# A decoder step on one core: last output in two token halves, dt copied as its output ends, C projected from token 12

## The chip, the cores and the metric

One Trainium2 chip, one of its cores. The metric is the device time of one execution in microseconds; the kernel before has a median of 880.47 over 3 runs (879.78 to 883.48).

## The reference, cut to what matters

One layer of a hybrid decoder for 304 tokens: 16 learned meta tokens, 256 prompt tokens and 8 sample sequences of 4 tokens. `mix` stands for the short gated convolution (branch A) and the state-space scan (branch B), both fed by one input projection.

```
h = x + 0.5 * swiglu(rmsnorm(h0), w_gu1) @ w_down1
u = rmsnorm(h) @ w_in        # A_b | A_c | A_h | z | xBC | dt | gate_A | gate_B
xbc = silu(causal_dwconv4(xBC) + bias)     # x: 16 tiles of channels, B: 4, C: 4
h = h + mix(u) @ w_o
h = h + 0.5 * swiglu(rmsnorm(h), w_gu2) @ w_down2
y = rmsnorm(h)               # without the meta tokens
```

D is 1024 (8 tiles of 128 channels), the hidden width 2816 (22 tiles). The rows of C for the 16 meta tokens are read only by the convolution (width 4) of the tokens behind them: no output for a meta token is wanted, and the scan reads C from token 16.

## The kernel before, in words

Channels lie on partitions and tokens along the free axis. Every weight tile of 128x128 is used once, in the order of a written list (`program`, line 68): an entry names a phase (`g1`, `dt`, `x`, `d2`, ...), an output tile m and a step k. `drive` (line 232) walks through it. Eight weight tiles make a unit that comes with one load on SP (`w_dma`, four units ahead) and is cast in two parts (`split_piece`, line 178, three units ahead): ScalarE writes `whi`, VectorE the rest `wlo`. Both are of a rounded fp32 type (fp32r), as the two parts of the activations are. Each entry is three matmuls (lines 255 to 257): high by high, high by low, low by high. They accumulate in one PSUM tile per output; the pool for these has four buffers (`psm`), another of four serves the scan and the norms (`pss`). When an output ends, its handler is called (`ev_x`, `ev_d`, ...). The order on each engine is set by a scheduler of the framework, which starts from the order of the program but may move instructions.

Beside the list runs `side`, a queue of generators that `drive` steps through at a rate per entry (`RATE1` 0.15 in the `x` phase). The dt output is handled there: its handler (line 593) only appends the generator `setup` (line 726), whose first step copies the PSUM tile to `dtraw` (line 735).

In the `x` phase outputs come in pairs, first B with C of a group, and `ev_x` (line 484) copies them to `cb`, convolves them (lines 495 to 499) and writes `xs`. Each matmul covers the columns in `spans`: 304 for `x`, 288 for phases that need no meta tokens.

The end: `d2` has 8 outputs of 22 steps each. `ev_d` (line 386) adds each to the residual stream `h` and calls `last_chunk` (line 684): a square and a running sum for the final norm (`square_chunk`), and `hn`, which is `h` times the norm's weight. For m=7 evict and square are done in two halves of 144 tokens. Behind the last matmul come two calls of `finish` (line 695; the sums over channels as plain fp32 matmuls, the root, two VectorE steps, in `rms`), five multiplications of `hn` by the norm (line 699) and five stores (line 700).

Of the kernel before, what the change touches and what calls it, by code (L numbers as in the profile page):

```python
# [34 lines left out]
XC = 16  # L35
XBC = XC + 2 * G
EPS = 1e-6
UT = 8
NWARM = 8
AHEAD = {"1": 2, "2": 1}  # L40
# [81 lines left out]
def tile_step(ctx: ExitStack, tc: tile.TileContext, wst: bass.AP, xT: bass.AP, vec: bass.AP,  # L122
# [102 lines left out]

    operands = {}
    spans = {}
    handlers = {}
    ps_t = {}
    wanted = {"rate": 0.0, "due": 0.0}  # L230

    def drive(ph_stop=None, m_stop=None):

        i = clock["i"]
        while i < len(PROGRAM):
            e = PROGRAM[i]
            if e[1] == ph_stop and (m_stop is None or e[2] == m_stop):
                break
            if e[0] == "mm":
                _, ph, m, k, first, last = e  # L240
                t = clock["t"]
                u, s = divmod(t, UT)
                if s == 0:
                    w_dma(u + LD)
                    w_split(u + LS)
                c0, c1 = spans[ph]
                if first:

                    pl, tag = (pss, "s") if ph in ("g1", "u1") and m == AHEAD["1"] else (psm, "m")
                    ps_t[ph, m] = pl.tile([P, 512], F32, name=f"ps_{ph}{m}", tag=tag)  # L250
                o = ps_t[ph, m][:, :c1 - c0]
                wh = hi_t[u][:, s * P:(s + 1) * P]
                wl = lo_t[u][:, s * P:(s + 1) * P]
                xh, xl = operands[ph](m, k)
                te.matmul(o, lhsT=wh, rhs=xh, start=first, stop=False)  # L255
                te.matmul(o, lhsT=wh, rhs=xl, start=False, stop=False)  # L256
                te.matmul(o, lhsT=wl, rhs=xh, start=False, stop=last)  # L257
                clock["t"] = t + 1
                run_due()
                wanted["due"] = min(wanted["due"] + wanted["rate"], 1.0 * len(side))  # L260
                while wanted["due"] >= 1.0:
                    wanted["due"] -= 1.0
                    side_step()
            else:
                _, ph, m = e
                c0, c1 = spans[ph]
                handlers[ph](m, ps_t.pop((ph, m))[:, :c1 - c0])
            i += 1
        clock["i"] = i
# [89 lines left out]
            return [q[:, k, c0:] for q in un]  # L359


    def ffn(i, norm, fp, hook, parts=None):

        c0, n = norm.c0, norm.n
        parts = parts or ((0, n),)
        spans.update({"g" + i: (c0, T), "u" + i: (c0, T), "d" + i: (c0, T)})
        hh = fp.tile([P, FC, n], F32R, name="hh" + i)
        hl = fp.tile([P, FC, n], F32R, name="hl" + i)
        sg = {}

        def ev_g(j, ps):
            s = fp.tile([P, n], F32, name=f"sg{i}_{j}", tag="sg", bufs=2)
            q = fp.tile([P, n], F32, name=f"sgr{i}_{j}", tag="hid", bufs=2)
            dve.tensor_tensor(out=q, in0=ps, in1=norm.r, op=ALU.mult)
            act.activation(s, q, AF.Silu)
            dve.tensor_tensor(out=s, in0=s, in1=norm.r, op=ALU.mult)
            sg[j] = s

        def ev_u(j, ps):
            s = sg.pop(j)  # L380
            q = fp.tile([P, n], F32, name=f"hid{i}_{j}", tag="hid", bufs=2)
            dve.tensor_tensor(out=q, in0=ps, in1=s, op=ALU.mult)
            act.activation(hh[:, j, :], q, AF.Copy)
            dve.tensor_tensor(out=hl[:, j, :], in0=q, in1=hh[:, j, :].bitcast(F32), op=ALU.subtract)

        def ev_d(m, ps):
            for a, b in parts if m == DC - 1 else ((0, n),):
                o = h[:, m, c0 + a:c0 + b]
                dve.scalar_tensor_tensor(out=o, in0=ps[:, a:b], scalar=0.5, in1=o, op0=ALU.mult, op1=ALU.add)
                hook(m, a, b)  # L390

        operands["g" + i] = operands["u" + i] = lambda m, k: norm.get(True, k, c0)
        operands["d" + i] = lambda m, k: (hh[:, k, :], hl[:, k, :])
        handlers["g" + i], handlers["u" + i], handlers["d" + i] = ev_g, ev_u, ev_d
# [89 lines left out]
    def ev_x(m, ps):  # L484
        b = cb[len(pair)]
        sb = blocks(b, 3 + S0, 7)
        act.activation(b[:, 3:3 + S0], ps[:, 0:S0], AF.Copy)
        act.activation(sb[:, :, 3:7], blocks(ps, S0, NT), AF.Copy)
        pool.tensor_copy(sb[:, :, 0:3], hs_t[:, m])
        c = xp.tile([P, CW], F32, name=f"cv{m}", tag="cv", bufs=4)  # L490
        pair.append((m, b, c))
        if len(pair) < 2:
            return
        for m, b, c in pair:
            act.activation(c[:, :CN], b[:, 0:CN], AF.Copy, scale=vcol(V_CW + 4 * m))
        for q in range(1, 4):
            for m, b, c in pair:
                dve.scalar_tensor_tensor(out=c[:, :CN], in0=b[:, q:q + CN], scalar=vcol(V_CW + 4 * m + q),
                                         in1=c[:, :CN], op0=ALU.mult, op1=ALU.add)
        for m, b, c in pair:  # L500
            pool.tensor_copy(ocs[:, m], tails(b, S0, 7, 3))
        both = list(pair)
        pair.clear()
# [1 line left out]
        cb.append(cb.pop(0))  # L505

        def last():
            for m, b, c in both:
                bias = vcol(V_CB + m)
                act.activation(xs[:, m, 0:S0], c[:, 0:S0], AF.Silu, bias=bias)  # L510
                act.activation(blocks(xs[:, m, :], S0, NT), blocks(c, 3 + S0, 7)[:, :, 0:NT], AF.Silu, bias=bias)
            ssd.bc = ssd.bc or both[1][0] == 1
        after(1, last)
# [56 lines left out]
                  "ga": (NM, T), "ya": (NM, T), "z": (NM, T), "gb": (NM, T), "yb": (NM, T), "wo": (NM, T)})  # L570
    for ph in ("x", "dt", "ac", "ah", "ab", "ga", "z", "gb"):
        def op(m, k, ph=ph):
            return nmx.get(ph == "ga" and m < nraw, k, spans[ph][0])
        operands[ph] = op
    operands["ya"] = lambda m, k: (ya[0][:, k, :], ya[1][:, k, :])
    drive("dt")
# [13 lines left out]


    ssd = Scan(tc, mp, pss, dram, xs, V, K, h0, o_hp, o_hs)
    dt_box["fn"] = lambda ps: side.append(ssd.setup(ps, xp))
    wanted["rate"] = RATE1
    drive("ac")
    run_due(True)
# [86 lines left out]

    def last_chunk(m, a, b):
        nf.chunk(m, a, b)
        if b == TM:
            act.activation(hn[:, m, :], h[:, m, NM:], AF.Copy, scale=vcol(V_NF + m))

    halves = ((0, TM // 2), (TM // 2, TM))
    ffn("2", n2, fp, last_chunk, halves)  # L690
    drive()
    run_due(True)

    for a, b in halves:
        nf.finish(a, b)

    for i, (m0, m1) in enumerate(((0, 1), (1, 2), (2, 4), (4, 6), (6, DC))):
        o = hn[:, m0:m1, :]
        dve.tensor_tensor(out=o, in0=o, in1=nf.r.unsqueeze(1).to_broadcast([P, m1 - m0, TM]), op=ALU.mult)
        (nc.scalar if i % 2 else nc.sync).dma_start(o_y[:, m0:m1], o)  # L700
    f_st.close()
    raw_st.close()
    h_st.close()
# [2 lines left out]
class Scan:  # L706
# [16 lines left out]
        self.n += 1  # L723
        return self.sp.tile(shape, dt, name=f"{name}_{self.n}", tag=tag or name, bufs=bufs)

    def setup(self, psd, xp):

        nc, K, V = self.nc, self.K, self.V  # L730
        te, act, dve, pool = nc.tensor, nc.scalar, nc.vector, nc.gpsimd
        ident = K[:, C_ID:C_ID + P]
        raw = xp.tile([P, T], F32, name="dtraw")
        reps = xp.tile([P, 2, P], F32, name="dtrep")
        act.activation(raw, psd, AF.Copy)  # L735
        act.activation(reps[:, 0].rearrange("p (k t) -> p k t", t=NL),
                       raw[:, TL:S0].unsqueeze(1).to_broadcast([P, P // NL, NL]), AF.Copy)
        act.activation(reps[:, 1].rearrange("p (k t) -> p k t", t=NB * NT),
# [502 lines left out]
```

## Time and profile before

| | |
|---|---|
| median of 3 runs | 880.47 us |
| profiled execution, its own time | 881.86 us |
| span of the profiled execution | 880.0 us |
| TensorE matmuls busy | 868.8 us (99%) |
| VectorE busy | 621.3 us (71%) |
| ScalarE busy | 496.2 us (56%) |
| mean granted clock of TensorE | 0.996 |

The span runs from the first to the last instruction of the profiled execution. In rows, PE is a matmul on TensorE, PEld its weight load, DVE is VectorE, ACT ScalarE, SPq and ACTq the issue of DMAs. L257 is line 257 of the kernel. Matmuls overlap, so a row shows one longer than the distance to the next.

### The profile page before, as it was taken

What the parts mean: (1) busy time and instruction counts of PE and PEld (TensorE: products, weight loads), DVE (VectorE), ACT (ScalarE), POOL (GpSimd) and SP (SyncE); (2) the same over time, 40 slices, a digit from 0 to 9 for tenths busy, and PEclk for the clock granted to TensorE, in tenths of its full rate; (3) what the DMA queues carried; (4) which work ended last, traced back from release to release, by engine and by line L of the source; (5) the groups of instructions that cost most, each with busy time, mean ns of one, the idle gap of its engine ahead of it and who ended that gap; (6) DMA issues with size and microseconds to landing.
All of it is one profiled execution on the core that took longest, in us unless ns stands there. A gap on an engine that the chain in (4) does not pass through costs nothing.

```text
span 880.0 us, 16239 instructions
## 1 busy us (share of the span) xinstructions
PE 868.8 (99%) x6448; PEld 849.8 (97%) x6448; DVE 621.3 (71%) x996; ACT 496.2 (56%) x899; POOL 53.4 (6%) x86
## 2 busy tenths in 40 slices
PE   9999999999999999999999999999999999999996
PEld 7999999999999999999999899999999999999996
DVE  6756666554677798799988999886676666665443
ACT  8543434343667787966655687774465444444442
POOL 0000000000012233001000211100000000000000
PEclk9999999999999999999999999999999999999999
DMA  8554545454644545865666655755555555555541
GB/s 299 190 155 157 165 147 167 146 166 150 201 166 146 153 153 171 314 211 202 231 223 225 242 198 174 257 183 169 167 168 166 164 165 166 163 164 168 169 139 54
DMA packets 45851, 158.69 MB, mean 180 GB/s; under 512 B 7168, under 2 KB 9504, under 8 KB 43472
## 3 DMA queue, kind: packets, MB, share of 16 engines
q1 hardware_dynamic: 45344, 157.21, 54.6%
q8 instruction: 50, 0.82, 0.4%
q10 hardware_dynamic: 432, 0.46, 0.2%
q14 instruction: 25, 0.20, 0.1%
HBM read 145.34 MB, written 12.31 MB: 179 GB/s over the span
## 4 chain that ended last, share of the span: by engine, by line
PE 97%; DVE 1%; ACT 1%; DMA 1%; SPq 0%; issue 0%; DVEq 0%
PE ps_d L257 6%; PE ps_d L256 5%; PE ps_d L255 5%; PE ps_u L257 5%; PE ps_g L255 5%; PE ps_u L256 5%; PE ps_u L255 5%; PE ps_g L257 5%; PE ps_g L256 5%; PE ps_x L255 3%; PE ps_x L256 3%; PE ps_x L257 3%; PE ps_z L255 2%; PE ps_z L257 2%; PE ps_yb L257 2%; PE ps_yb L255 2%
## 5 line engine op out<-in xcount | busy, mean ns | idle before, releaser
L184 DVE TENSOR_TENSOR wlo<-wraw,whi 128x1024 fp32r<-128x1024 f32 (+2 forms) x250 | 300.6, 1204 | 188.8 <-ACT whi L183 188.1
L183 ACT ACTIVATE whi<-wraw 128x1024 fp32r<-128x1024 f32 (+2 forms) x250 | 259.6, 1041 | 296.8 <-issue 182.8
L257 PE MATMUL ps_d<-hh,wlo 128*128 128x304 f32 (+1 forms) x352 | 105.6, 300 | 0.0
L255 PE MATMUL ps_d<-hh,whi 128*128 128x304 f32 (+1 forms) x352 | 105.0, 299 | 0.0
L256 PE MATMUL ps_d<-hl,whi 128*128 128x304 f32 (+1 forms) x352 | 104.7, 298 | 0.0
L256 PEld LDWEIGHTS ps_d<-hl,whi 128*128 128x128 f32 x352 | 66.7, 189 | 0.0
L257 PEld LDWEIGHTS ps_d<-hh,wlo 128*128 128x128 f32 x352 | 66.2, 188 | 0.0
L255 PEld LDWEIGHTS ps_d<-hh,whi 128*128 128x128 f32 x352 | 66.1, 188 | 0.0
L255 PE MATMUL ps_x<-unh,whi 128*128 128x304 f32 x192 | 58.8, 309 | 0.7 <-ACT dtraw L735 0.7
L256 PE MATMUL ps_x<-unl,whi 128*128 128x304 f32 x192 | 58.8, 307 | 0.0
L257 PE MATMUL ps_x<-unh,wlo 128*128 128x304 f32 x192 | 58.6, 306 | 0.0
L255 PE MATMUL ps_g<-n1h,whi 128*128 128x304 f32 x176 | 54.1, 308 | 0.7 <-ACT whi L183 0.7
L256 PE MATMUL ps_u<-n1l,whi 128*128 128x304 f32 x176 | 53.6, 304 | 0.0
L255 PE MATMUL ps_u<-n1h,whi 128*128 128x304 f32 x176 | 53.5, 304 | 0.0
L256 PE MATMUL ps_g<-n1l,whi 128*128 128x304 f32 x176 | 53.4, 304 | 0.0
L257 PE MATMUL ps_g<-n1h,wlo 128*128 128x304 f32 x176 | 53.1, 303 | 0.0
L257 PE MATMUL ps_u<-n1h,wlo 128*128 128x304 f32 x176 | 52.9, 302 | 0.0
L257 PE MATMUL ps_g<-n2h,wlo 128*128 128x288 f32 x176 | 52.3, 297 | 0.0
L255 PE MATMUL ps_u<-n2h,whi 128*128 128x288 f32 x176 | 52.2, 297 | 0.0
L257 PE MATMUL ps_u<-n2h,wlo 128*128 128x288 f32 x176 | 52.1, 296 | 0.0
L255 PE MATMUL ps_g<-n2h,whi 128*128 128x288 f32 x176 | 51.9, 295 | 0.0
L256 PE MATMUL ps_u<-n2l,whi 128*128 128x288 f32 x176 | 51.4, 292 | 0.0
(342 smaller groups left out, 2435.6 us busy)
## 6 DMA issues: line engine op xcount, KB each, us to landing
wraw<-wst SPq DMA_DIRECT2D x241, 512.0 KB, 3.5
h<-h SPq DMA_DIRECT2D x8, 1024.0 KB, 5.0
o_hs<-h SPq DMA_DIRECT2D x8, 1024.0 KB, 4.3
acb<-cumd SPq DMA_DIRECT2D x8, 512.0 KB, 4.3
wraw<-wst SPq DMA_DIRECT2D x7, 256.0 KB, 6.4
hd<-h SPq DMA_DIRECT2D x1, 1216.0 KB, 6.6
h<-hd SPq DMA_DIRECT2D x1, 1216.0 KB, 8.3
o_hp<-hf SPq DMA_DIRECT2D x8, 128.0 KB, 2.8
```

The source lines that it names most:

```text
L183: act.activation(hi[:, a:b], r[:, a:b], AF.Copy)
L184: dve.tensor_tensor(out=lo[:, a:b], in0=r[:, a:b], in1=hi[:, a:b].bitcast(F32), op=ALU.subtract)
L255: te.matmul(o, lhsT=wh, rhs=xh, start=first, stop=False)
L256: te.matmul(o, lhsT=wh, rhs=xl, start=False, stop=False)
L257: te.matmul(o, lhsT=wl, rhs=xh, start=False, stop=last)
```

## The change

- The last output (`d2`, m=7) is made in two halves of the tokens: 66 matmuls of 144 columns for the first, then 66 for the second, from the same weight tiles, which are kept, into a PSUM tile of its own. After six of the 22 steps of the second half `out(0, TH)` is called: norm, two multiplications and two stores (both on SP) for the first half. Behind the last matmul come the norm, four multiplications and four stores for the second half.
- The handler of dt copies the PSUM tile to `dtraw` itself; the generator starts with the copy.
- The four outputs for C cover the columns from token 12 (292 instead of 304); copies, convolution and activation of these are cut to match.

```diff
--- before.py
+++ after.py
@@ -35,6 +35,7 @@
 XC = 16
 XBC = XC + 2 * G
 EPS = 1e-6
+C0 = NM - 4
 UT = 8
 NWARM = 8
 AHEAD = {"1": 2, "2": 1}
@@ -225,9 +226,20 @@
 
     operands = {}
     spans = {}
+
+    def span(ph, m):
+        return (C0, T) if ph == "x" and m >= XC + G else spans[ph]
+
     handlers = {}
     ps_t = {}
+    byhalf = {}
     wanted = {"rate": 0.0, "due": 0.0}
+
+    def three(o, ws, xs, cols, first, last):
+        (wh, wl), (xh, xl) = ws, [x[:, cols] for x in xs]
+        te.matmul(o, lhsT=wh, rhs=xh, start=first, stop=False)
+        te.matmul(o, lhsT=wh, rhs=xl, start=False, stop=False)
+        te.matmul(o, lhsT=wl, rhs=xh, start=False, stop=last)
 
     def drive(ph_stop=None, m_stop=None):
 
@@ -243,7 +255,19 @@
                 if s == 0:
                     w_dma(u + LD)
                     w_split(u + LS)
-                c0, c1 = spans[ph]
+                c0, c1 = span(ph, m)
+                if (ph, m) in byhalf:
+
+                    (a, b), kept = byhalf[ph, m]
+                    if first:
+                        ps_t[ph, m] = psm.tile([P, 512], F32, name=f"ps_{ph}{m}a", tag="m")
+                    ws = [t[u][:, s * P:(s + 1) * P] for t in (hi_t, lo_t)]
+                    kept.append((ws, operands[ph](m, k)))
+                    three(ps_t[ph, m][:, a:b], *kept[-1], slice(a, b), first, last)
+                    clock["t"] = t + 1
+                    run_due()
+                    i += 1
+                    continue
                 if first:
 
                     pl, tag = (pss, "s") if ph in ("g1", "u1") and m == AHEAD["1"] else (psm, "m")
@@ -263,7 +287,7 @@
                     side_step()
             else:
                 _, ph, m = e
-                c0, c1 = spans[ph]
+                c0, c1 = span(ph, m)
                 handlers[ph](m, ps_t.pop((ph, m))[:, :c1 - c0])
             i += 1
         clock["i"] = i
@@ -359,10 +383,8 @@
             return [q[:, k, c0:] for q in un]
 
 
-    def ffn(i, norm, fp, hook, parts=None):
-
+    def ffn(i, norm, fp, hook):
         c0, n = norm.c0, norm.n
-        parts = parts or ((0, n),)
         spans.update({"g" + i: (c0, T), "u" + i: (c0, T), "d" + i: (c0, T)})
         hh = fp.tile([P, FC, n], F32R, name="hh" + i)
         hl = fp.tile([P, FC, n], F32R, name="hl" + i)
@@ -383,11 +405,10 @@
             act.activation(hh[:, j, :], q, AF.Copy)
             dve.tensor_tensor(out=hl[:, j, :], in0=q, in1=hh[:, j, :].bitcast(F32), op=ALU.subtract)
 
-        def ev_d(m, ps):
-            for a, b in parts if m == DC - 1 else ((0, n),):
-                o = h[:, m, c0 + a:c0 + b]
-                dve.scalar_tensor_tensor(out=o, in0=ps[:, a:b], scalar=0.5, in1=o, op0=ALU.mult, op1=ALU.add)
-                hook(m, a, b)
+        def ev_d(m, ps, a=0, b=n):
+            o = h[:, m, c0 + a:c0 + b]
+            dve.scalar_tensor_tensor(out=o, in0=ps[:, a:b], scalar=0.5, in1=o, op0=ALU.mult, op1=ALU.add)
+            hook(m, a, b)
 
         operands["g" + i] = operands["u" + i] = lambda m, k: norm.get(True, k, c0)
         operands["d" + i] = lambda m, k: (hh[:, k, :], hl[:, k, :])
@@ -484,20 +505,21 @@
     def ev_x(m, ps):
         b = cb[len(pair)]
         sb = blocks(b, 3 + S0, 7)
-        act.activation(b[:, 3:3 + S0], ps[:, 0:S0], AF.Copy)
-        act.activation(sb[:, :, 3:7], blocks(ps, S0, NT), AF.Copy)
+        a = span("x", m)[0]
+        act.activation(b[:, 3 + a:3 + S0], ps[:, 0:S0 - a], AF.Copy)
+        act.activation(sb[:, :, 3:7], blocks(ps, S0 - a, NT), AF.Copy)
         pool.tensor_copy(sb[:, :, 0:3], hs_t[:, m])
         c = xp.tile([P, CW], F32, name=f"cv{m}", tag="cv", bufs=4)
-        pair.append((m, b, c))
+        pair.append((m, b, c, a and a + 3))
         if len(pair) < 2:
             return
-        for m, b, c in pair:
-            act.activation(c[:, :CN], b[:, 0:CN], AF.Copy, scale=vcol(V_CW + 4 * m))
+        for m, b, c, a in pair:
+            act.activation(c[:, a:CN], b[:, a:CN], AF.Copy, scale=vcol(V_CW + 4 * m))
         for q in range(1, 4):
-            for m, b, c in pair:
-                dve.scalar_tensor_tensor(out=c[:, :CN], in0=b[:, q:q + CN], scalar=vcol(V_CW + 4 * m + q),
-                                         in1=c[:, :CN], op0=ALU.mult, op1=ALU.add)
-        for m, b, c in pair:
+            for m, b, c, a in pair:
+                dve.scalar_tensor_tensor(out=c[:, a:CN], in0=b[:, q + a:q + CN], scalar=vcol(V_CW + 4 * m + q),
+                                         in1=c[:, a:CN], op0=ALU.mult, op1=ALU.add)
+        for m, b, c, a in pair:
             pool.tensor_copy(ocs[:, m], tails(b, S0, 7, 3))
         both = list(pair)
         pair.clear()
@@ -505,9 +527,9 @@
         cb.append(cb.pop(0))
 
         def last():
-            for m, b, c in both:
+            for m, b, c, a in both:
                 bias = vcol(V_CB + m)
-                act.activation(xs[:, m, 0:S0], c[:, 0:S0], AF.Silu, bias=bias)
+                act.activation(xs[:, m, a:S0], c[:, a:S0], AF.Silu, bias=bias)
                 act.activation(blocks(xs[:, m, :], S0, NT), blocks(c, 3 + S0, 7)[:, :, 0:NT], AF.Silu, bias=bias)
             ssd.bc = ssd.bc or both[1][0] == 1
         after(1, last)
@@ -570,7 +592,7 @@
                   "ga": (NM, T), "ya": (NM, T), "z": (NM, T), "gb": (NM, T), "yb": (NM, T), "wo": (NM, T)})
     for ph in ("x", "dt", "ac", "ah", "ab", "ga", "z", "gb"):
         def op(m, k, ph=ph):
-            return nmx.get(ph == "ga" and m < nraw, k, spans[ph][0])
+            return nmx.get(ph == "ga" and m < nraw, k, span(ph, m)[0])
         operands[ph] = op
     operands["ya"] = lambda m, k: (ya[0][:, k, :], ya[1][:, k, :])
     drive("dt")
@@ -590,7 +612,13 @@
 
 
     ssd = Scan(tc, mp, pss, dram, xs, V, K, h0, o_hp, o_hs)
-    dt_box["fn"] = lambda ps: side.append(ssd.setup(ps, xp))
+
+    def ev_dt(ps):
+        raw = xp.tile([P, T], F32, name="dtraw")
+        act.activation(raw, ps, AF.Copy)
+        side.append(ssd.setup(raw, xp))
+
+    dt_box["fn"] = ev_dt
     wanted["rate"] = RATE1
     drive("ac")
     run_due(True)
@@ -683,21 +711,39 @@
 
     def last_chunk(m, a, b):
         nf.chunk(m, a, b)
-        if b == TM:
-            act.activation(hn[:, m, :], h[:, m, NM:], AF.Copy, scale=vcol(V_NF + m))
-
-    halves = ((0, TM // 2), (TM // 2, TM))
-    ffn("2", n2, fp, last_chunk, halves)
+        act.activation(hn[:, m, a:b], h[:, m, NM + a:NM + b], AF.Copy, scale=vcol(V_NF + m))
+
+    def out(a, b, queues, pieces):
+
+        nf.finish(a, b)
+        for i, (m0, m1) in enumerate(pieces):
+            o = hn[:, m0:m1, a:b]
+            dve.tensor_tensor(out=o, in0=o, in1=nf.r[:, a:b].unsqueeze(1).to_broadcast([P, m1 - m0, b - a]), op=ALU.mult)
+            queues[i % len(queues)].dma_start(o_y[:, m0:m1, a:b], o)
+
+
+
+    last, TH, BEHIND = ("d2", DC - 1), TM // 2, 5
+    kept = []
+    byhalf[last] = ((0, TH), kept)
+    ffn("2", n2, fp, last_chunk)
+    ends = handlers["d2"]
+
+    def ev_last(m, ps):
+        if m < DC - 1:
+            return ends(m, ps)
+        ends(m, ps, 0, TH)
+        p2 = psm.tile([P, 512], F32, name="ps_d2b", tag="m")
+        for i, w in enumerate(kept):
+            three(p2[:, TH:TM], *w, slice(TH, TM), i == 0, i == FC - 1)
+            if i == BEHIND:
+                out(0, TH, [nc.sync], ((0, 4), (4, DC)))
+        ends(m, p2, TH, TM)
+
+    handlers["d2"] = ev_last
     drive()
     run_due(True)
-
-    for a, b in halves:
-        nf.finish(a, b)
-
-    for i, (m0, m1) in enumerate(((0, 1), (1, 2), (2, 4), (4, 6), (6, DC))):
-        o = hn[:, m0:m1, :]
-        dve.tensor_tensor(out=o, in0=o, in1=nf.r.unsqueeze(1).to_broadcast([P, m1 - m0, TM]), op=ALU.mult)
-        (nc.scalar if i % 2 else nc.sync).dma_start(o_y[:, m0:m1], o)
+    out(TH, TM, [nc.sync, nc.scalar], ((0, 2), (2, 4), (4, 6), (6, DC)))
     f_st.close()
     raw_st.close()
     h_st.close()
@@ -723,16 +769,14 @@
         self.n += 1
         return self.sp.tile(shape, dt, name=f"{name}_{self.n}", tag=tag or name, bufs=bufs)
 
-    def setup(self, psd, xp):
+    def setup(self, raw, xp):
 
 
 
         nc, K, V = self.nc, self.K, self.V
         te, act, dve, pool = nc.tensor, nc.scalar, nc.vector, nc.gpsimd
         ident = K[:, C_ID:C_ID + P]
-        raw = xp.tile([P, T], F32, name="dtraw")
         reps = xp.tile([P, 2, P], F32, name="dtrep")
-        act.activation(raw, psd, AF.Copy)
         act.activation(reps[:, 0].rearrange("p (k t) -> p k t", t=NL),
                        raw[:, TL:S0].unsqueeze(1).to_broadcast([P, P // NL, NL]), AF.Copy)
         act.activation(reps[:, 1].rearrange("p (k t) -> p k t", t=NB * NT),
```

## Rows read from the trace of the kernel before

**Rows 1.** page, busy time of each engine and granted clock in 40 slices

```profile
PE 868.8 (99%) x6448; PEld 849.8 (97%) x6448; DVE 621.3 (71%) x996; ACT 496.2 (56%) x899; POOL 53.4 (6%) x86
...
PEclk9999999999999999999999999999999999999999
```

**Rows 2.** waits of TensorE over the whole span: us in total, times, longest

```profile
PE ps_x L255 <- ACT dtraw L735: 0.7, 1, 0.7
```

**Rows 3.** timeline, first and last of the 66 matmuls of the last output

```profile
861.53 0.29 PE L255 MATMUL ps_d<-hh,whi 128*128 128x288 f32 x1
...
870.12 0.30 PE L257 MATMUL ps_d<-hh,wlo 128*128 128x288 f32 x1
```

**Rows 4.** timeline behind the last matmul

```profile
870.25 0.65 PE L280 MATMUL nf_ss<-nf_acc,K 128*128 128x144 f32 x4
870.46 0.52 DVE L389 SCALAR_TENSOR_TENSOR h<-ps_d,h 128x144 f32<-128x144 f32 x2 [6.77 <-PE ps_d L257]
870.80 0.54 ACT L335 ACTIVATE nf_sq<-h 128x144 f32<-128x144 f32 x2 [6.19 <-DVE h L389]
...
871.72 0.65 ACT L282 ACTIVATE nf_acc<-nf_ss,K 128x144 f32<-128x144 f32 x2
...
873.73 2.83 DVE L699 TENSOR_TENSOR hn<-hn,rr 128x288 f32<-128x288 f32 x5
```

**Rows 5.** DMA issues of 870 to 880 us: count, KB each, us to landing

```profile
o_y<-hn SPq DMA_DIRECT2D x2, 288.0 KB, 2.2
...
o_y<-hn ACTq DMA_DIRECT2D x1, 144.0 KB, 1.8
```

**Rows 6.** timeline, matmuls of 32 columns with loads of 128 columns

```profile
279.21 0.30 PEld L784 LDWEIGHTS sps<-dta,gtl 16*128 16x128 f32 x2
279.24 0.38 PE L784 MATMUL sps<-dta,gtl 16*128 16x32 f32 x2
279.43 0.30 PEld L785 LDWEIGHTS sps<-dta,K 32*128 32x128 f32 x2
279.46 0.38 PE L785 MATMUL sps<-dta,K 32*128 32x32 f32 x2
```

**Rows 7.** timeline, a load of the rounded type after a wait, and the next

```profile
7.47 0.19 PEld L255 LDWEIGHTS ps_g<-n1h,whi 128*128 128x128 f32 x1 [0.56 <-ACT whi L183]
...
7.58 0.19 PEld L256 LDWEIGHTS ps_g<-n1l,whi 128*128 128x128 f32 x1
```

**Rows 8.** groups by form, 870 to 880 us: busy us, mean ns of one

```profile
L282 ACT ACTIVATE nf_acc<-nf_ss,K 128x144 f32<-128x144 f32 x2 | 0.7, 377 | 0.0
L284 DVE SCALAR_TENSOR_TENSOR rr<-nf_ss,K,rr 128x144 f32<-128x144 f32 x2 | 0.6, 363 | 1.6 <-ACT rr L283 1.6
...
L283 ACT ACTIVATE rr<-nf_acc 128x144 f32<-128x144 f32 x2 | 0.5, 320 | 0.0
...
L285 DVE SCALAR_TENSOR_TENSOR rr<-rr,nf_acc 128x144 f32<-128x144 f32 x2 | 0.5, 298 | 0.0
```

**Rows 9.** timeline, matmuls of 304 columns; the first and the seventh start

```profile
277.70 0.30 PE L255 MATMUL ps_x<-unh,whi 128*128 128x304 f32 x1
...
278.54 0.30 PE L781 MATMUL sps<-dta,K 128*128 128x32 f32 x2
```

**Rows 10.** timeline around the copy of dt

```profile
252.07 2.01 ACT L183 ACTIVATE whi<-wraw 128x1024 fp32r<-128x1024 f32 x2 [2.91 <-issue]
...
252.66 0.30 PE L257 MATMUL ps_dt<-unh,wlo 128*128 128x304 f32 x1
...
253.16 2.36 DVE L184 TENSOR_TENSOR wlo<-wraw,whi 128x1024 fp32r<-128x1024 f32 x2 [3.43 <-ACT whi L183]
...
253.49 0.29 PE L256 MATMUL ps_ga<-unl,whi 128*128 128x288 f32 x1
253.98 0.41 ACT L735 ACTIVATE dtraw<-ps_dt 128x304 f32<-128x304 f32 x1
...
254.44 0.41 PE L255 MATMUL ps_x<-unh,whi 128*128 128x304 f32 x1 [0.66 <-ACT dtraw L735]
```

## The prediction

> **What bounds the kernel now.** I read the page first: TensorE is busy for 868.8 of 880.0 us and its granted clock is at 9 tenths or more in every slice [rows 1]. So the time is the number of matmuls times the distance from one start to the next, plus what lies behind the last matmul. Next, the waits of TensorE: the longest single one inside the work is 0.7 us, before a matmul into `ps_x`, for the copy of dt [rows 2]. There is almost no idle time to win; only fewer or shorter matmuls, or a shorter end, can help.
>
> Then the last output, d2 of m=7: 66 matmuls of 288 columns, the first at 861.53, the last at 870.12 [rows 3]. That is 8.59 us over 65 steps, 0.132 us each. A row shows 0.29 to 0.30 for a single one since they overlap; the distance of starts is what counts.
>
> Last, the end: 9.88 us from the start of the last matmul to 880.00. Its chain runs: evict 870.46, square 870.80, first root 871.72, first multiplication by the norm 873.73, the last of these ends at 873.73 + 2.83 = 876.56 [rows 4], and then a store, which takes 2.2 us to land for a large piece [rows 5].
>
> **The change part by part**
>
> *1. Twice the matmuls of half the width.* The 66 matmuls of 288 columns become 132 of 144, and every one keeps its own 128x128 weight load. Half the columns would be half the time only if the load hides behind 144 columns. No matmul of this type with 144 columns is in the trace, so I go to the nearest rows. Small matmuls with 32 columns behind loads of 128 columns: two loads start at 279.21 and two at 279.43, and their matmuls keep that step, at 279.24 and 279.46 [rows 6]. That is 0.22 us for two, 0.11 for one, though 32 columns are next to nothing to stream: there the load sets the pace. They are plain fp32, but the load of the weights used here behaves alike: after a wait, the load at 7.47 is followed by the next at 7.58, again 0.11 [rows 7]. In the steady stream the load shows because 0.132 is longer than 0.11. With 144 columns, about 0.066 if the columns alone set it, it would.
>
> So I take 0.111 as the distance. The bounds: 0.066 below (columns alone) and 0.132 above (nothing gained by fewer columns). 131 steps of 0.111 are 14.54 us in place of 8.59: **+5.95**. The Trainium skill, in "TensorE: Matmul & The Clock Gate", section "Back-to-back issue gap", gives about 81 ns for each pair of load and matmul at 128 columns in a sustained stream. As an estimate by that figure, 131 steps would be 10.6 us, part 1 would be +2.0 and the sum below -0.7. The row of 0.11 at 32 columns speaks against it.
>
> *2. The norm of the first half among the matmuls.* After six of the 22 steps of the second half the two sums for the norm are put in, four passes of 144 columns each. Before, four such passes took 0.65 from the first start to the last end [rows 4]; with 0.29 for the last one, three steps are 0.36, 0.12 each: 4 x 0.12 = **+0.5** on TensorE, which is now in front of the last matmul. Is there a wait too? The squares they need are ready after evict and square, some 0.28 + 0.34 to the start of the square and about 0.4 for it, 1.0 us in all, behind the first half's last matmul, and 18 matmuls x 0.111 = 2.0 us stand between: no wait. The bounds are 0 (the sums fall where TensorE stands anyway) and 1.0.
>
> What rides on the other engines is covered. VectorE's and ScalarE's work for the half takes some 1.5 us, the two multiplications about 1.5 (2304 columns took 2.83 [rows 4], so 1152 take 1.4 and a little), and the two stores on SP, with no weight load queued behind them, some 2 us more. All that starts 2.5 us into 7.3 us of matmuls. VectorE is free again about 1.5 us before the second half's evict; the store lands about when the matmuls end. Without that cover the evict would be late by what is over.
>
> *3. The end, for one half.* From last matmul to evict 0.34 becomes 0.28 (144 fewer columns to run through, 0.06); evict to square 0.34 and square to root 0.92 stay. Between the first root (871.72) and the first multiplication (873.73) lie 2.01 us with four steps done for both halves [rows 4]. Done once, they last 0.377 + 0.320 + 0.363 + 0.298 [rows 8] = 1.36, with four hand-overs of 0.04 (870.42 to 870.46 at the evict) 1.5: -0.5. The multiplications cover 1152 columns instead of 2304, about 1.5 instead of 2.83: -1.3. The last store is 144 KB, which landed in 1.8 us where 288 KB took 2.2 [rows 5]: -0.4. Together -0.06 - 0.5 - 1.3 - 0.4, **-2.2** (bounds -1.6, if strided halves and the store cost more, and -2.6).
>
> *4. C from token 12.* Four outputs x 8 x 3 = 96 matmuls have 292 columns instead of 304. At 304 seven starts go from 277.70 to 278.54, 0.140 each [rows 9]; at 288 it is 0.132, so 0.0005 per column and 96 x 12 x 0.0005 = 0.58, taken as **-0.5** (bounds 0 and -0.6). The convolutions are 12 columns shorter on engines that are not the bound: nothing. For the same reason nothing comes from the copies, the square or the casts of part 2.
>
> *5. dt copied at its end.* The dt output ends at 252.66 + 0.30; its copy waits behind two weight casts and starts at 253.98; the matmul that takes over its PSUM buffer starts at 254.44 rather than 253.49 + 0.13 = 253.62 [rows 10]. So 0.8 us are lost. The copy moves ahead of a cast, which gets later by 0.41 on ScalarE; the weights behind it are casts ahead of their use. What is late next is the low half of the current weights: `ps_ga` L257 needs the first of two VectorE pieces that run from 253.16 for 2.36, thus about 254.34; it would come up at some 254.1 and stand 0.3. I take **-0.5**; the bounds are 0 and -0.8.
>
> Sum: 5.95 + 0.5 - 2.2 - 0.5 - 0.5 = **+3.25 us**, a span of 883.2. The profiled execution took 881.86, 1.86 around its span of 880.0; the median of the runs, 880.47, is 1.39 below it. I add the difference to the median: **883.7 us**, +0.37%. About 0.5%, here 4.4 us, is what a measurement can tell from no change, so the forecast is "same" on the slower side, and values above 884.9 count as slower. Its own range, from the bounds of parts 2 to 5 and a distance of 0.109 to 0.116, is 882.2 to 885.5.
>
> **The rivals**
>
> *The loads hide (chance 0.11).* If the next load starts early enough, columns alone set the pace: 131 x 0.066 = 8.65, part 1 is +0.06 and the sum -2.6: 877.8 us, still within 0.5%. For it: at 288 columns loads hide completely, no idle shows. Against it: the 0.11 between loads in both groups [rows 6, 7]. The rule of the Trainium skill cited above ("Back-to-back issue gap") would land in between, at 879.8 by the estimate, and its chance is within these 0.11.
>
> *Narrow matmuls pay the full step (0.08), slower.* The place is the step of the 132 matmuls; the price is a distance of 0.132 as at 288: 131 x 0.132 = 17.3, part 1 +8.7, sum +6.0: 886.5 us. From a distance of 0.120 on it decides for slower. For it: a first matmul after a gap already stands for load plus start; against it: steps of 0.11 are in the trace.
>
> *Narrow matmuls run at the plain fp32 rate (0.05), slower.* A plain fp32 matmul takes two passes of 0.12 for 144 columns [rows 4]. At 0.242 each, 131 steps are 31.7, part 1 +23.1, sum +20.4: 900.9 us. Nothing shows that the width changes the rate, but no narrow one of this type is there.
>
> *The change does not do what it says (0.06), slower.* The first half's norm could be ordered behind the second half: the order on the engines is not the program's (both accumulator sums ran at 870.25, ahead of the first square's [rows 4]). Then parts 2 and 3 go: 5.95 - 0.5 - 0.5 = +4.95: 885.4 us.
>
> **How the numbers follow.** The forecast has 0.70; of that about 0.14 lies above 884.9, its last half microsecond, and 0.56 is same. Slower: 0.14 + 0.08 + 0.05 + 0.06 = 0.33. The rival with hidden loads gives 0.09 same and, with every bound at its good end, 0.02 faster. Same is 0.65. The range goes from 881.8 to 887.0: it takes in the forecast, the full step and the norm that sinks (0.84), and leaves out the hidden loads and the fp32 rate.
>
> **What would show it.** The starts of the d2 matmuls of m=7: 0.11 apart, some 14.5 us from first to last. The first half's `o_y` stores issued before the last matmul. From last matmul to span end about 7.7 us instead of 9.9. No wait of `ps_x` for `dtraw`, perhaps 0.3 at `ps_ga`. Starts of the C matmuls 0.134 apart. The prediction is wrong if the matmuls of 144 columns are 0.07 or over 0.12 apart, if TensorE waits before the sums, if the granted clock falls during the narrow matmuls, or if the reordered stage of `ps_x` gains or loses over 1 us elsewhere.

## The result and the profile after

The kernel after takes 885.89 us (median of 6 runs, 885.5 to 886.19), the kernel before 881.32 (6 runs, 879.78 to 883.48). The ratio is 1.0051 with a 95% interval of 1.0037 to 1.0064: slower by 0.51%, where +0.37% was forecast. That is inside the stated range of 881.8 to 887.0, and above the forecast's own of 882.2 to 885.5. The three runs of before that came with the result moved its median up by 0.85 from the 880.47 the forecast was added to. The profiled executions took 885.71 and 881.86; their spans are 883.9 and 880.0.

First the page of after, beside [rows 1]: TensorE is busy for 5.1 us more, for 66 more matmuls, and only the last slice of the clock, behind the last matmuls, is lower.

```profile
PE 873.9 (99%) x6514; PEld 854.8 (97%) x6514; DVE 622.1 (70%) x997; ACT 496.6 (56%) x900; POOL 47.1 (5%) x86
...
PEclk9999999999999999999999999999999999999998
```

Next the timeline of the last output in after (start, duration, engine, line, operation): the first, third and fourth matmul of the first half, the last of it, the first of the second, and the last. Beside [rows 3].

```profile
860.88 0.23 PE L240 MATMUL ps_d27a<-hh,whi 128*128 128x144 f32 x1
...
861.06 0.27 PE L242 MATMUL ps_d27a<-hh,wlo 128*128 128x144 f32 x1
...
861.17 0.27 PE L240 MATMUL ps_d27a<-hh,whi 128*128 128x144 f32 x1
...
868.10 0.28 PE L242 MATMUL ps_d27a<-hh,wlo 128*128 128x144 f32 x1
...
868.21 0.28 PE L240 MATMUL ps_d2b<-hh,whi 128*128 128x144 f32 x1
...
875.96 0.28 PE L242 MATMUL ps_d2b<-hh,wlo 128*128 128x144 f32 x1
```

From 860.88 to 875.96 are 15.07 us unrounded for 131 steps; before it was 8.59 for 65. The first step, behind the last matmul of 288 columns, is 0.07; the others are 0.11 (their median is 0.112), and the change from one PSUM tile to the other costs nothing (868.10 to 868.21).

Among them stand the sums of the first half's norm. TensorE in after, 870 to 871.6 us:

```profile
870.11 0.28 PE L242 MATMUL ps_d2b<-hh,wlo 128*128 128x144 f32 x1
870.22 0.45 PE L304 MATMUL nf_ss<-nf_acc,K 128*128 128x144 f32 x2
...
870.57 0.27 PE L241 MATMUL ps_d2b<-hl,whi 128*128 128x144 f32 x1
...
871.25 0.45 PE L304 MATMUL nf_ss<-nf_sq,K 128*128 128x144 f32 x2
```

No row has a wait in brackets. From 870.11 to 870.57 are 0.46 where two steps of 0.11 would be 0.22; the same again at 871.25. So the sums cost 2 x 0.244 = 0.49 us; the 14.58 that are left of the 15.07 are 0.111 for each of 131 steps.

Then the end, beside [rows 4]. VectorE, ScalarE and the DMA issues of after from 873 us on:

```profile
873.25 1.43 DVE L721 TENSOR_TENSOR hn<-hn,rr 128x576 f32<-128x576 f32 x2
...
874.03 6.61 SPq L722 DMA_DIRECT2D o_y<-hn  x4
...
876.27 0.31 DVE L410 SCALAR_TENSOR_TENSOR h<-ps_d2b,h 128x144 f32<-128x144 f32 x1 [1.59 <-PE ps_d2b L242]
876.61 0.32 ACT L359 ACTIVATE nf_sq<-h 128x144 f32<-128x144 f32 x1 [4.14 <-DVE h L410]
...
877.54 0.38 ACT L306 ACTIVATE nf_acc<-nf_ss,K 128x144 f32<-128x144 f32 x1 [0.30 <-PE nf_ss L304]
...
879.05 1.56 DVE L721 TENSOR_TENSOR hn<-hn,rr 128x288 f32<-128x288 f32 x4
```

The first half's two multiplications (873.25 to 874.68) and the first of its stores (874.03) run before the last matmul at 875.96: that part of the change does what it says. The second of these stores lands at 877.6, 1.6 us behind the last matmul and well before the next store is issued (879.5). Behind the last matmul the chain is that of one half: from root (877.54) to multiplication (879.05) it takes the four steps of [rows 8] once each, 1.51 us. The span ends 7.97 us after the last matmul instead of some 9.9.

The stores of after, 866 to 884 us (issues, KB each, median us to landing), beside [rows 5]:

```profile
DMA packets 2145, 1.20 MB, mean 66 GB/s; under 512 B 96, under 2 KB 2144, under 8 KB 2144
...
o_y<-hn SPq DMA_DIRECT2D x2, 288.0 KB, 2.7
o_y<-hn SPq DMA_DIRECT2D x2, 144.0 KB, 2.0
o_y<-hn ACTq DMA_DIRECT2D x2, 144.0 KB, 2.2
```

One by one, the four stores of 144 KB land in 1.9, 2.0, 2.2 and 2.3 us, in the order of their issue.

Last the copy of dt. Waits of TensorE in after, beside [rows 2], and the timeline around the copy, beside [rows 10]:

```profile
PE ps_x L279 <- ACT dtraw L618: 0.7, 1, 0.7
```

```profile
251.89 2.01 ACT L184 ACTIVATE whi<-wraw 128x1024 fp32r<-128x1024 f32 x2 [2.80 <-issue]
...
252.47 0.30 PE L281 MATMUL ps_dt<-unh,wlo 128*128 128x304 f32 x1
...
253.81 0.41 ACT L618 ACTIVATE dtraw<-ps_dt 128x304 f32<-128x304 f32 x1
...
254.26 0.41 PE L279 MATMUL ps_x<-unh,whi 128*128 128x304 f32 x1 [0.69 <-ACT dtraw L618]
```

The copy has another line number and the same place: behind two weight casts, 1.0 us after dt ends (252.77 to 253.81). All of this stage is earlier by 0.2 (0.06 since the start of `ps_x`, the rest by narrower matmuls of C), and the wait is still 0.7.

**The stages.** Single spans differ by more than an experiment has to tell: in some executions TensorE is granted half its clock for 3.4 us near 282 us, which takes 1.5 us (last section), and the first 16 us vary. So the runs below are compared by stages, read as starts in the timelines: stage I from the first matmul into `ps_x` to the first into `ps_ac`; stage II from the first to the last matmul of d2 m=7; stage III from there to the span's end. Between I and II lie 513.6 us in every kernel but whole, which takes 514.15.

| kernel | I | half clock near 282 us | II | III | II + III |
|---|---|---|---|---|---|
| before | 104.06 | yes | 8.59 | 9.85 | 18.44 |
| after | 103.48 | yes | 15.07 | 7.97 | 23.04 |
| whole | 102.01 | no | 8.59 | 9.85 | 18.44 |
| oldc | 102.54 | no | 15.07 | 7.98 | 23.05 |
| cut216 | 103.51 | yes | 15.27 | 7.01 | 22.28 |
| load64 | 103.54 | yes | 12.29 | 8.42 | 20.71 |
| endhalf | 102.01 | no | 8.59 | 11.09 | 19.68 |
| wide | 103.52 | yes | 15.07 | 7.64 | 22.71 |
| wholedt | 103.09 | yes | 8.59 | 9.97 | 18.56 |
| endwide | 101.57 | no | 8.59 | 10.09 | 18.68 |

Between before and after: up to stage I 0.06 less, stage I 0.58 less, II 6.48 more, III 1.89 less (unrounded); together +3.95, the difference of the spans (880.0 and 883.9). The medians differ by 4.57, with 3.3 to 5.6 as the interval (0.0037 and 0.0064 of 881.32): the profiled execution of before stood 0.54 above its median, that of after 0.18 below.

### The profile page after: what moved, and what is told of

The parts are those of the page before. It is cut to its first block, busy times and chain, and to the rows that moved or that the text cites. A ratio compares the mean times of both kernels' runs of the same rounds, so it can differ in the third digit from the quotient of the medians.

```text
span 883.9 us, 16371 instructions
## 1 busy us (share of the span) xinstructions
PE 873.9 (99%) x6514; PEld 854.8 (97%) x6514; DVE 622.1 (70%) x997; ACT 496.6 (56%) x900; POOL 47.1 (5%) x86
## 4 chain that ended last, share of the span: by engine, by line
PE 97%; DVE 1%; ACT 1%; issue 1%; DMA 0%; SPq 0%; DVEq 0%
PE ps_u L281 5%; PE ps_g L279 5%; PE ps_u L280 5%; PE ps_u L279 5%; PE ps_g L281 5%; PE ps_g L280 5%; PE ps_d L281 5%; PE ps_d L280 5%; PE ps_d L279 5%; PE ps_x L279 3%; PE ps_x L281 3%; PE ps_x L280 3%; PE ps_z L279 2%; PE ps_z L281 2%; PE ps_yb L281 2%; PE ps_yb L279 2%
## 5 line engine op out<-in xcount | busy, mean ns | idle before, releaser
L281 PE MATMUL ps_d<-hh,wlo 128*128 128x304 f32 (+1 forms) x330 | 99.1, 300 | 0.0
L279 PE MATMUL ps_d<-hh,whi 128*128 128x304 f32 (+1 forms) x330 | 98.5, 299 | 0.0
L280 PE MATMUL ps_d<-hl,whi 128*128 128x304 f32 (+1 forms) x330 | 98.3, 298 | 0.0
L280 PEld LDWEIGHTS ps_d<-hl,whi 128*128 128x128 f32 x330 | 62.5, 189 | 0.0
L281 PEld LDWEIGHTS ps_d<-hh,wlo 128*128 128x128 f32 x330 | 62.1, 188 | 0.0
L279 PEld LDWEIGHTS ps_d<-hh,whi 128*128 128x128 f32 x330 | 62.0, 188 | 0.0
L279 PE MATMUL ps_x<-unh,whi 128*128 128x304 f32 (+1 forms) x192 | 58.1, 306 | 0.7 <-ACT dtraw L618 0.7
L281 PE MATMUL ps_x<-unh,wlo 128*128 128x304 f32 (+1 forms) x192 | 58.4, 305 | 0.0
L280 PE MATMUL ps_x<-unl,whi 128*128 128x304 f32 (+1 forms) x192 | 58.2, 304 | 0.0
```

## The experiments

**whole: the last output in one piece again, dt and C as in the kernel after.**

```diff
     def ev_last(m, ps):
-        if m < DC - 1:
-            return ends(m, ps)
-        ends(m, ps, 0, TH)
...
+        for a, b in halves if m == DC - 1 else ((0, TM),):
+            ends(m, ps, a, b)
...
-    out(TH, TM, [nc.sync, nc.scalar], ((0, 2), (2, 4), (4, 6), (6, DC)))
+    for a, b in halves:
+        nf.finish(a, b)
+    for i, (m0, m1) in enumerate(((0, 1), (1, 2), (2, 4), (4, 6), (6, DC))):
...
```

> The changed kernel with its last output whole again (66 matmuls of 288 columns, the end of the kernel before); dt and C stay as changed. Theory (the doubled weight loads cost the time): everything up to the last output is as in the changed kernel, 0.65 us ahead of before, and the last output and the end cost what they did before, so a span of 879.3 against 880.0 before and 883.9 changed, about 0.1% faster than before. Rival (the new order of the x stage or the cuts cost time that shows at the end): a span of 880 or more.

Measured: 880.88 us (12 runs), ratio to before 0.9991 (0.9979 to 1.0003). The profiled execution, without the half clock, spans 877.9. Stages II and III are those of before. So the whole loss of the kernel after lies in the split of the last output: 23.04 - 18.44 = 4.6 us. What is left of the change, C and dt together, is a gain of about 0.1%, 0.2% at most, that this measurement does not tell from none.

**oldc: C over all 304 columns again, the rest as in the kernel after.**

```diff
-C0 = NM - 4
+C0 = 0
```

> The kernel after with one part undone: the four outputs for C cover all 304 columns again; halves and dt as in the kernel after. If the 12 columns fewer are what the stage gained, the stretch from the first matmul into ps_x to the first into ps_ac is 104.06 us again as in the kernel before (102.6 where the half clock near 282 us is missing), 0.58 longer than in the kernel after, and the 96 matmuls of C stand 0.005 to 0.006 us further apart. Rival: the gain came from the moved dt copy or from another hand-over, and C is hidden; then the stretch stays at 103.48 (102.0 without the half clock). The last output is as in the kernel after, 15.07 us from first to last matmul and 7.97 behind it.

Measured: 884.17 us (one run, before beside it 881.83). No half clock near 282 us, stage I 102.54 where 102.6 was expected; next to whole, which has none either, it is 0.53 longer. So the gain of stage I comes from C and not from dt. The median distance of starts is 0.140 us for 304 columns in both, and 0.134 for the 292 of C in whole and in after. The first matmuls into `ps_x` and `ps_ac`, in oldc and then in whole:

```profile
243.18 0.30 PE L279 MATMUL ps_x<-unh,whi 128*128 128x304 f32 x1
...
345.72 0.30 PE L279 MATMUL ps_ac<-unh,whi 128*128 128x290 f32 x1
```

```profile
243.32 0.30 PE L279 MATMUL ps_x<-unh,whi 128*128 128x304 f32 x1
...
345.33 0.30 PE L279 MATMUL ps_ac<-unh,whi 128*128 128x290 f32 x1
```

**cut216: the cut at token 216 instead of 144.** The last output has 66 matmuls of 216 columns and 66 of 72.

```diff
-    last, TH, BEHIND = ("d2", DC - 1), TM // 2, 5
+    last, TH, BEHIND = ("d2", DC - 1), 216, 5
```

> The changed kernel with the cut at token 216 of 288 instead of 144. Theory (a load of 128 columns sets the step whatever the columns are, up to some 240): matmuls of 216 and of 72 columns both 0.111 us apart, first to last start 15.1 us as at 144, and a shorter end for 72 tokens, 0.7 us less in the multiplications: a span of 883.0 to 883.3. Rival (the step has a fixed part and a part per column, on a line through 0.111 at 144 and 0.132 at 288): 0.121 apart in the first part and 0.101 in the second, with the same sum.

Measured: 884.57 us (one run). TensorE in both parts, from the timeline of cut216:

```profile
861.16 0.28 PE L240 MATMUL ps_d27a<-hh,whi 128*128 128x216 f32 x1
861.27 0.27 PE L241 MATMUL ps_d27a<-hl,whi 128*128 128x216 f32 x1
...
875.22 0.28 PE L240 MATMUL ps_d2b<-hh,whi 128*128 128x72 f32 x1
875.33 0.28 PE L241 MATMUL ps_d2b<-hl,whi 128*128 128x72 f32 x1
```

0.11 for 216 columns and 0.11 for 72, as for 144. The distance does not depend on the columns there. Stage II is 0.20 longer than in the kernel after although the columns are the same in all: the norm's sums for 216 columns show 388 ns a pass instead of 308. Stage III is about 1 us shorter, since only 72 tokens are left for it. Both together win 0.8 of the 4.6 us.

**load64: the second half's matmuls with loads of 64 columns.**

```diff
-            three(p2[:, TH:TM], *w, slice(TH, TM), i == 0, i == FC - 1)
+            (wh, wl), xq = w
+            three(p2[0:64, TH:TM], (wh[:, 0:64], wl[:, 0:64]), xq, slice(TH, TM), i == 0, i == FC - 1)
```

> The changed kernel, but the matmuls of the second half load 64 weight columns instead of 128 and make only channels 0 to 63 of the last output: the update of channels 64 to 127 for these tokens is left out. Theory (the load sets the step, and lasts in proportion to its columns): the step of the second half falls from 0.111 to 0.066 to 0.075, 66 of them 2.4 to 3.0 us less, a span of 880.9 to 881.5. Rival (a floor for each matmul of this type, whatever it loads): 0.111 as before, a span of 883.9.

Measured: 882.88 us (one run). TensorE in the first and in the second half, from the timeline of load64, and the other engines at its end:

```profile
866.05 0.27 PE L240 MATMUL ps_d27a<-hh,whi 128*128 128x144 f32 x1
866.16 0.28 PE L241 MATMUL ps_d27a<-hl,whi 128*128 128x144 f32 x1
...
867.54 0.19 PEld L242 LDWEIGHTS ps_d27a<-hh,wlo 128*128 128x128 f32 x1
...
870.93 0.14 PEld L241 LDWEIGHTS ps_d2b<-hl,whi 128*64 128x64 f32 x1
...
871.00 0.23 PE L241 MATMUL ps_d2b<-hl,whi 128*64 128x144 f32 x1
...
871.13 0.23 PE L240 MATMUL ps_d2b<-hh,whi 128*64 128x144 f32 x1
...
872.11 1.43 DVE L721 TENSOR_TENSOR hn<-hn,rr 128x576 f32<-128x576 f32 x2
...
873.46 0.29 DVE L743 SCALAR_TENSOR_TENSOR h<-ps_d2b,h 64x144 f32<-64x144 f32 x1
```

Same columns, half the load: a median of 0.068 instead of 0.112 (from 871.00 to 871.13 are two steps, L241 to L242 to L240), and the row of a load is 0.14 instead of 0.19. Together with cut216 this settles that the tokens that stream past do not set the pace of the narrow matmuls: the pace stays with 72, 144 or 216 of them, and quickens with fewer columns in the load. load64 also makes half the output channels, which go with the load's columns. That it is the load is the reading that [rows 7] suggests, where a load starts 0.11 behind the one before; a run that parts the two was not made. With 64 columns the load may no longer be what sets the step: 0.066 was the estimate for 144 columns alone. A by-product was not expected: with the second half 2.8 us shorter, VectorE is still at the first half's multiplications (872.11 + 1.43 = 873.54) when the second half ends, and its evict starts as they end, at 873.46. Stage III is 8.42 instead of 7.97. This is the cover of part 2 gone: it cost 0.45 here.

**endhalf: matmuls whole, but the end multiplied and stored by halves.** Can the gain at the end be had without the narrow matmuls?

```diff
+    for (a, b), pieces in zip(halves, (((0, 4), (4, DC)), ((0, 2), (2, 4), (4, 6), (6, DC)))):
+        nf.finish(a, b)
+        for i, (m0, m1) in enumerate(pieces):
+            o = hn[:, m0:m1, a:b]
...
+            (nc.scalar if i % 2 else nc.sync).dma_start(o_y[:, m0:m1, a:b], o)
```

> As the run with the last output whole, but behind the last matmul the first half of the tokens is normed, multiplied and stored before the second half is multiplied. Theory (most of what the end gained came from handling one half at a time with smaller stores, and needs no second set of matmuls): the multiplications start up to 0.5 us earlier than before and the last store is of 144 KB, so 0.5 to 0.9 us below the run with the last output whole, a span of 878.4 to 878.8, 0.1 to 0.2% faster than before. Rival (the end is only shorter because the first half lies beside matmuls): the same span as with the last output whole, 879.3, or longer by up to 0.5 for the smaller store pieces.

Measured: 881.08 us (12 runs), ratio 1.0 (0.9988 to 1.0012). Stage III is 11.09, longer than the 9.85 of before. The timeline of endhalf and its stores:

```profile
870.59 0.64 DVE L308 SCALAR_TENSOR_TENSOR rr<-nf_ss,K,rr 128x144 f32<-128x144 f32 x2 [1.89 <-ACT rr L307]
...
871.58 2.90 DVE L731 TENSOR_TENSOR hn<-hn,rr 128x576 f32<-128x576 f32 x6
```

```profile
DMA packets 2144, 1.18 MB, mean 66 GB/s; under 512 B 96, under 2 KB 2144, under 8 KB 2144
...
o_y<-hn SPq DMA_DIRECT2D x1, 288.0 KB, 2.6
o_y<-hn ACTq DMA_DIRECT2D x1, 288.0 KB, 2.9
o_y<-hn SPq DMA_DIRECT2D x2, 144.0 KB, 3.2
o_y<-hn ACTq DMA_DIRECT2D x2, 144.0 KB, 3.3
```

The theory of an early first half fell, and the loss of 1.24 against whole (19.68 and 18.44 for II + III) is more than the 0.5 of the rival. Each step runs for both halves in turn ("x2" in one row), so the first half is ready no earlier than both together, and the stores of half the tokens move in 2144 packets where the whole ones of [rows 5] are fewer and larger (720 in whole): the last ones land 3.2 to 3.3 us after their issue, against 1.8 to 2.2 before.

**wide: the kernel after with `hn` and the output laid out by halves.** The tokens of a half stand together for all m, so that a store of two m has 1152 bytes in a row instead of 576 twice.

```diff
-    hn = fp.tile([P, DC, TM], F32, name="hn")
+    hn = fp.tile([P, 2, DC, TM // 2], F32, name="hn")
...
-            queues[i % len(queues)].dma_start(o_y[:, m0:m1, a:b], o)
+            queues[i % len(queues)].dma_start(o_y[:, s, m0:m1], o)
```

> The changed kernel with hn and the output laid out by halves, so that a store of two channel tiles moves rows of 1152 bytes instead of two of 576. Theory (the end fell short of the forecast because small pieces land later): the last store lands in about 1.8 us instead of 2.2, the stretch from the first matmul of the last output to the span's end goes from 23.0 to 22.5 to 22.7. Rival (piece size does not matter, the four stores wait for each other on the way): 23.0 as before.

Measured: 884.89 us (one run). The stores of wide:

```profile
DMA packets 865, 1.20 MB, mean 66 GB/s; under 512 B 96, under 2 KB 608, under 8 KB 864
...
o_y<-hn SPq DMA_DIRECT2D x2, 288.0 KB, 2.1
o_y<-hn SPq DMA_DIRECT2D x2, 144.0 KB, 1.8
o_y<-hn ACTq DMA_DIRECT2D x2, 144.0 KB, 1.9
```

The same bytes in 865 packets instead of 2145; the 144 KB land in 1.7 to 1.9, about the price of [rows 5], and stage III is 0.33 shorter (7.64). The rival keeps a remainder: the last of the four stores still takes 0.18 longer than the first, where in after it takes 0.36 longer.

**wholedt: whole, and the copy of dt on VectorE instead of ScalarE.**

```diff
     def ev_dt(ps):
         raw = xp.tile([P, T], F32, name="dtraw")
-        act.activation(raw, ps, AF.Copy)
+        dve.tensor_copy(raw, ps)
```

> As the run with the last output whole, but dt is copied on VectorE, which is idle when dt ends, instead of ScalarE, which has two weight casts ahead of it. Theory (the changed kernel left the copy where it was, behind the casts, so its part could gain nothing; the wait is worth something): the wait of ps_x for dtraw goes, and of its 0.8 us some 0.3 to 0.5 remain as a gain because the low half of the weights is late next. Rival (the low half is then later by the copy, and takes all of it back): no change to the run with the last output whole.

Measured: 879.9 us (12 runs), ratio to before 0.999 (0.998 to 1.0). The copy in the timeline of wholedt, and the matmul that waited for it:

```profile
254.88 0.30 PE L281 MATMUL ps_dt<-unh,wlo 128*128 128x304 f32 x1
...
255.22 0.47 DVE L618 COPY dtraw<-ps_dt 128x304 f32<-128x304 f32 x1 [3.13 <-PE ps_dt L281]
...
256.37 0.41 PE L279 MATMUL ps_x<-unh,whi 128*128 128x304 f32 x1 [0.15 <-ACT whi L184]
```

On VectorE, which had been idle for 3.13 us, the copy starts 0.04 us after dt ends. The wait of 0.7 is gone; one of 0.15, for a weight cast that is late, stands in its place. Stage I is 103.09 against 103.48 in the kernel after, both with the half clock, and 101.57 (endwide) against 102.01 (whole) without: 0.39 and 0.44 us. This is what part 5 of the change was forecast to bring.

**endwide: endhalf with the layout of wide and dt on VectorE.**

```diff
+            s = 2 * a // TM
+            o = hn[:, s, m0:m1]
...
+            (nc.scalar if i % 2 else nc.sync).dma_start(o_y[:, s, m0:m1], o)
```

> As the run with dt on VectorE, and the end by halves as in the run of that kind, with hn and the output laid out by halves. Theory (the end by halves lost 1.2 us to small pieces alone): the stretch from the first matmul of the last output to the span's end goes from 19.7 to 18.0 to 18.3, 0.2 to 0.4 below the 18.4 of the whole stores. Rival (six stores instead of five cost it, whatever their pieces): 19 or more.

Measured: 880.58 us, ratio 0.9991 (0.9982 to 1.0001). Stage III is 10.09 instead of 11.09 in endhalf: one microsecond by the layout alone, and still no gain over stores of all tokens (9.85). II + III is 18.68, neither the 18.0 to 18.3 of the theory nor the 19 of the rival. Of the 0.24 above whole, 0.13 lies ahead of the first multiplication, 0.06 in the multiplications and 0.05 behind them. Endwide is no better than wholedt, the lowest median of all here. Against after, wholedt is faster (0.998 to 1.0 of before, where after has 1.0037 to 1.0064); against before it is faster by 0.2% at most.

## Why the prediction was right

- **Part 1, the narrow matmuls (+5.95): right in mechanism and size.** 0.111 us per step against 0.111, 14.58 us for 131 steps against 14.54. (The prediction's "in the steady stream the load shows" says the reverse of what it argues from: at 288 columns the load does not show, because 0.132 is longer than 0.11.) The nearest rows, loads of 128 columns before 32 columns [rows 6] and after a wait [rows 7], gave the price of a matmul that no row showed. cut216 and load64 bear the cause out: the distance stays with 72, 144 or 216 columns and falls with a load of 64. The rivals "the loads hide" (0.066), "full step" (0.132) and "plain fp32 rate" (0.242) all fell by this number. The Trainium skill, "TensorE: Matmul & The Clock Gate", gives about 81 ns at 128 columns in "Back-to-back issue gap". The 0.11 measured here at 72, 144 and 216 columns differs, and the measurement decides. The same page, in "LDWEIGHTS (loading the stationary operand)", gives a load as its columns over 1.2 in ns, by which an estimate for 128 columns is 107. The measured 0.11 agrees.
- **Part 2, the sums among the matmuls (+0.5): right.** 0.49, with no wait, and the first half's work lay beside the matmuls: VectorE was free 1.59 us before the second evict, for "about 1.5". So the rival in which the first half's norm sinks behind the second half fell. The store landed 1.6 us later than "about when the matmuls end", which held nothing up. load64 shows that the cover, which the forecast named, is real: where it was gone, the evict came late and stage III took 0.45 more.
- **Part 3, the end (-2.2): right in its chain, -1.9 in size; the step that failed is the last store.** Evict, square and root came out within 0.03. From root to multiplication 1.51 were measured for 1.5, and the multiplications took 1.56 for "about 1.5". The forecast priced the last store, of 144 KB, at 1.8, as [rows 5] have it, -0.4. It landed in 2.3, as the last one of 288 KB does in before, and from the end of the last multiplication to the end of the span are 3.3 us where before it was 3.4, -0.1. The row priced a store of the same bytes in longer runs, issued first and not last; wide, with 1152 bytes in a row, gets the last one down to 1.9 and 0.33 back. The bound of -1.6 was there for this.
- **Part 4, C from token 12 (-0.5): right.** -0.58 between before and after, -0.53 between oldc and whole; the distance fell from 0.140 to 0.134.
- **Part 5, dt (-0.5): wrong.** The step that failed is "the copy moves ahead of a cast". The copy was issued earlier in the program and ran in the old place: the scheduler put it behind the same two casts (80 casts of weights precede it on ScalarE in both kernels, where the order of the program in after has 78), and the wait is 0.7 as in [rows 2]. The value of 0.5 was about right, as wholedt shows with 0.4, and so was the lower bound of 0, which is what happened. The prediction named this risk, that the order on the engines is not the program's, for the norm, where it did not come, and not for dt, where it did.
- **The sum.** Forecast 3.25, measured in the spans 3.95: 0.03 from parts 1 and 2, 0.3 from the end, 0.5 from dt, -0.1 from C, -0.06 from the start. The time is 2.2 above the forecast: those 0.7, then 0.85 by which the median of before moved with more runs, and 0.6 by which the two profiled executions stand differently to their medians (the runs of before are a mixture, see the last section). So "within 0.5%" was the likeliest class, and the result lies on its edge, its interval on both sides. The forecast's own upper end, 885.5, which the measured time exceeds, was summed wrong: by its bounds, 6.6 + 1.0 - 1.6 = 6.0 make 886.5.

What stays open: whether the norm of a first part could be hidden behind a few narrow steps at the end alone, with most of the matmuls kept whole; it wasn't tried on the chip.

## What to carry to other kernels

In a row of matmuls here that each brought their own 128 weight columns, the distance did not fall below 0.11 us, down to 72 tokens. Before splitting a matmul by its moving columns, look in the trace for the shortest steady distance between two loads, and count the extra loads at that price (here 66 x 0.11 against an end shorter by 1.9). An instruction that is moved in the program has moved only if the trace says so; where an engine's order is set by a scheduler, moving the work to an engine that stood idle is what took the wait away here. A store's price is taken from one with the same run of bytes, not only the same size.

## What the runs showed of the hardware that was not expected

In six of the ten profiled executions (before, after, cut216, load64, wide, wholedt) the granted clock of TensorE is at its lower level, 1.2 GHz, for some 3.4 us around 282 us; in whole, oldc, endhalf and endwide it is not. In wholedt and endwide it is there for 3.4 us near 12 us as well, and their `ps_x` starts at 246.2 and 246.5, in the others at 243.2 to 243.9. The stretch from 280 to 289 us in before, after and whole (busy us and instructions of PE, PEld, DVE, ACT and POOL; then granted clock, DMA share, GB/s):

```profile
280.00:289.00 9.00, 9.00 (x62) 8.76 (x62) 3.58 (x7) 4.92 (x11) 1.28 (x2) 0.81 0.43 138
```

```profile
280.00:289.00 9.00, 9.00 (x64) 8.49 (x64) 3.48 (x7) 5.22 (x14) 0.60 (x2) 0.81 0.42 120
```

```profile
280.00:289.00 9.00, 9.00 (x74) 8.71 (x74) 3.01 (x7) 6.93 (x17) 1.02 (x4) 1.00 0.38 108
```

A mean of 0.81 over 9 us is half the clock for (1 - 0.81) x 9 / 0.5 = 3.4 of them. TensorE gets through 62 to 64 matmuls in such a stretch, at 1.00 through 74. Between after and whole, equal up to here, stage I differs by 1.47 us (103.48 and 102.01). From 278.5 (before), 279.6 (after) and 279.1 (whole) on, TensorE works for over 3 us at the small matmuls that prepare dt (16 to 128 columns, some of them in [rows 6]), in all three. In before the clock falls at 282.5, just behind them, and in after at 282.1, among them. Why the clock falls in some executions and not in others the runs don't show. The mean clock of the runs fits: 22 runs of before beside whole and wide with 0.997 or more have spans of 877.7 to 879.3, 23 with 0.996 or less 879.3 to 882.5, and the six of after all have 0.996. So the medians of the two kernels differ by a part that is the clock's, and the 3.95 of the stages, taken at the same clock, is the better figure for the change. A difference of 1.5 us between two profiles of this kernel is no evidence for or against a change until this stretch has been looked at.
